# Where the sums of weight blocks are made, and how many pairs are multiplied without them

## The chip, the cores and the metric

The kernel runs on one core of one Trainium2 chip. The metric is the device time of one execution in microseconds (us): the median of several runs. One more execution was taken by the hardware profiler; times of single instructions are from it.

## The reference, cut to what matters

One step of a diffusion network with two layers. The first layer mixes tokens with a state-space scan (SSD), the second with differential attention of eight heads; behind each stands a channel mixer. There are 512 latent and 128 context tokens, so 640 columns in all, and 1024 channels. What this case touches is the channel mixer of the second layer:

```python
def conv_ffn(h, up_w, conv_w, conv_b, down_w):
    u = dwconv(h @ up_w, conv_w, conv_b)
    a, v = jnp.split(u, 2, axis=-1)
    return (jax.nn.silu(a) * v) @ down_w
```

`up_w` is 1024 x 5632: an `a` half and a `v` half of 2816 channels each. `dwconv` is a filter of three taps along the tokens, with a bias for each channel.

## The kernel before, in words

**Products.** Channels lie on the 128 partitions, tokens in the columns. A product of fp32 accuracy is made of three matmuls: weight and activation are each split in a rounded part (`whi`, `h..h`) and the rest (`wlo`, `h..l`), and hi x hi, hi x lo and lo x hi are added in PSUM. `split_w` (L327) makes the two parts of a weight: a copy on ScalarE (L277 is the helper of all ScalarE work), then a subtraction on VectorE (L283 the helper for two-input operations, L280 for those with a scalar as well). L286 is the helper of all matmuls.

**Weights** come in an order that `weight_units` (L1354) lists once for the whole program: units of up to 1024 columns, each loaded in one transfer on SP's queue into one of four `raw` buffers (L306). `nextw` (L332) hands out the next unit; it loads three units ahead and splits one ahead. A unit's split parts lie in one of five pairs of buffers in the second channel mixer.

**The second channel mixer.** A pair is one tile of 128 `a` channels and the tile of the same `v` channels; there are 22. A plain pair is two tiles of 8 contraction blocks x 3 matmuls x two column groups: 96 matmuls of 320 columns on average. From the fifth pair on (`STD = 4`) a pair is computed by class `Blocks` with seven block products in place of eight (Winograd's form): the two tiles of a pair are the rows, two halves of the contraction (four blocks each) the inner dimension, and two halves of the tokens (`HT` = 320 columns) the columns of a 2 x 2 block product. A product is 4 blocks x 3 matmuls, a pair 84 matmuls of 320 columns. Products 1 and 2 take weight blocks as they are, 4 also; 5, 6, 7 and 3 take sums of weight blocks. `product` (L152) runs one product, `pair` (L175) the seven of a pair, of which 3 and 4 are delayed into the next pair (`third`, `fourth`). The epilogue (L757) takes a pair's `ua` and `uv` through the filter, SiLU, product and split (`mh`, `ml`).

**What feeds the products.** The sums of activation blocks (`sums`, L61) are made by VectorE after the first plain pair, a few at a time: `hook` (L258) counts a tick for each contraction block and each block of a product, and lets waiting tasks go on. `finish_sums` (L93) stands after the last plain pair. The four sums of weight blocks of a pair are made by VectorE in `stage` (L119), from the pair's two loaded units; a plan (`plan`, L102) lists the products, and `stage` keeps the splits `LOOK = 7` products ahead of the product that runs.

**The order of the mixer.** Up pairs 0 to 7, the down projection of seven of them, pairs 8 to 14, the next down projection, pairs 15 to 21, the last. In the first of eight down tiles the last pair's products 3 and 4 are run (`between`, L210).

**Attention**, ahead of it, takes three tiles (q, k, v) for each head. `att_evac` (L1181) copies the context part of a head's keys into `kp`, of which there are two buffers; it is stored as an output (`kout`) and used by the head's scores. The head's normaliser goes through DRAM: `rsd` is written and comes back, spread over the partitions, as `rbc` (L400, L402). POOL has no work in this kernel.

Instructions of an engine run in the order in which the program lists them.

Of the kernel before, what the change touches and what calls it, by code (L numbers as in the profile page):

```python
# [41 lines left out]
STD = 4  # L42
HT = T // 2
LOOK = 7
# [5 lines left out]
class Blocks:  # L50


    def __init__(self, st, h, epilogue, pool):
        self.st, self.h, self.epilogue, self.pool = st, h, epilogue, pool
        self.ops = {}
        self.pend = None
        self.spare = None
        self.half = None
        self.units = sorted(st.paired)

    def sums(self):  # L61
# [5 lines left out]
        for j in range(4):  # L67
# [17 lines left out]
            for i, x in ((1, t1), (2, t2), (4, t4)):  # L85
# [3 lines left out]
                st.split_w(t[:, c1], t[:, c2], x)  # L89
# [3 lines left out]
    def finish_sums(self):  # L93
        st, h, t = self.st, self.h, self.t
        self.stage(LOOK)
# [6 lines left out]
    def plan(self, p0, p1):  # L102

        self.seq, self.done, self.at = [], 0, 0
        for p in range(p0, p1):
            prev = p > p0
            self.seq += [(1, p), (2, p)] + [(3, p - 1)] * prev + [(6, p)] + [(4, p - 1)] * prev + [(5, p), (7, p)]
        self.seq += [(0, p1 - 1), (3, p1 - 1), (4, p1 - 1)]

    def place(self):  # L110

        if self.half is None:
            hi, lo = self.st.parts()
            self.half = hi[:, 512:], lo[:, 512:]
            return hi[:, :512], lo[:, :512]
        o, self.half = self.half, None
        return o

    def stage(self, upto):  # L119

        st = self.st
        k1, k2 = slice(0, 512), slice(512, 1024)
        while self.done < min(upto, len(self.seq)):
            i, p = self.seq[self.done]
            self.done += 1
            if i == 0:
                self.half = None
                st.cast(self.units[2 * (p - STD)] + 2)
                continue
            o = self.ops.setdefault(p, {})  # L130
            if i == 1:
                u = self.units[2 * (p - STD)]
                st.prefetch(u + 1)
                x, y = st.wraw[u], st.wraw[u + 1]
                s = [self.pool.tile([P, 512], F32, tag=f"s{n}", name=f"s{n}_{p}", bufs=1) for n in range(1, 5)]
                st.tt(s[0], y[:, k1], y[:, k2], ALU.add)
                st.tt(s[1], s[0], x[:, k1], ALU.subtract)
                st.tt(s[2], x[:, k1], y[:, k1], ALU.subtract)
                o["raw"] = {1: x[:, k1], 2: x[:, k2], 4: y[:, k2], 5: s[0], 6: s[1], 7: s[2], 3: s[3]}
                if self.half is None:  # L140
                    hi, lo = st.parts()
                    st.split_w(hi, lo, x)
                    o[1], o[2] = ((hi[:, k], lo[:, k]) for k in (k1, k2))
            if i == 6:
                st.tt(o["raw"][3], o["raw"][2], o["raw"][6], ALU.subtract)
            if i not in o:
                o[i] = self.place()
                st.split_w(*o[i], o["raw"][i])

    B = {1: "11", 2: "21", 3: "22", 4: 4, 5: 1, 6: 2, 7: 3}  # L150
# [24 lines left out]
    def pair(self, p):  # L175
        st = self.st
        st.wi = self.units[2 * (p - STD)] + 2
        st.prefetch(st.wi + 1)
# [31 lines left out]
    def between(self, i, p0, p1):  # L210

        st = self.st
        if i == 0:
            self.third()
            self.fourth()
            self.half = self.spare = None
            if p1 > p0:
                self.plan(p0, p1)
        if i == 4:
            st.cast(st.wi + 2)  # L220
            self.stage(4)
        if i == 6:
            self.stage(LOOK)


class Step:


    def __init__(self, ctx, tc, a):
# [12 lines left out]
        self.paired = set()  # L242
        self.npart = 0
# [57 lines left out]
    def prefetch(self, upto):  # L301
        while len(self.wraw) <= min(upto, len(self.units) - 1):
            u = len(self.wraw)
            ap, n = self.units[u]
            r = self.pw.tile([P, 1024], F32, tag="raw", name=f"raw{u}", bufs=RAW)
            self.nc.sync.dma_start(r[:, :n], ap)  # L306
            self.wraw[u] = r

    def cast(self, upto):
        while len(self.wcast) <= min(upto, len(self.units) - 1):  # L310
            u = len(self.wcast)
            self.prefetch(u)
            if u in self.paired:
                self.wcast[u] = None
                continue
            n = self.units[u][1]
            hi, lo = (t[:, :n] for t in self.parts())
            self.split_w(hi, lo, self.wraw[u][:, :n])
            self.wcast[u] = hi, lo

    def parts(self):
        v = self.npart
        self.npart += 1
        wp, t, b = (self.pw, "w", 3) if self.px is None or v % 5 < 3 else (self.px, "x", 2)
        return [wp.tile([P, 1024], F32R, tag=t + nm, name=f"w{nm}{v}", bufs=b) for nm in ("hi", "lo")]

    def split_w(self, hi, lo, raw):  # L327

        self.act(hi, raw, AF.Copy)
        self.tt(lo, raw, hi.bitcast(F32), ALU.subtract)  # L330

    def nextw(self):  # L332
# [1183 lines left out]
```

## Time and profile before

| | |
|---|---|
| median of 3 runs | 1886.21 us (1880.86 to 1887.99) |
| the profiled execution | 1884.19 us |
| its span, first to last instruction | 1882.4 us |
| mean granted TensorE clock | 0.991 |
| TensorE (PE) busy | 1841.4 us, 98% |
| VectorE (DVE) busy | 1478.4 us, 79% |
| ScalarE (ACT) busy | 991.6 us, 53% |
| POOL busy | 0.2 us |
| moved by DMA | 209.72 MB, 111 GB/s in the mean |

Times in rows are us from the span's start. Attention stands at about 1060 to 1370, the second channel mixer from about 1390 to the end, its paired stages at 1466 to 1527, 1580 to 1666 and 1719 to 1805. A row of a group of instructions has the line, the engine, the operation, output<-inputs, their sizes and the count, then the busy time and the mean of one in ns, then the idle time ahead of them and what ended it. A row of the timeline has start, duration, engine, line, operation, and in brackets the wait ahead and what ended it. A row of a window has for each engine the busy time and, in brackets, the number of instructions; then the granted clock, the mean busy share of the 16 DMA engines, and what they moved. A row of DMA issues has the count, the size of one, and the median us from issue to landing.

### The profile page before, as it was taken

The page shows a single profiled execution, that of the slowest core. Times are in us where ns is not written, and L with a number is a line of the kernel's source. Part 1 is how long each engine was busy: PE and PEld are TensorE (multiplying, and loading weights), DVE is VectorE, ACT ScalarE, POOL GpSimd, SP SyncE. Part 2 cuts the span into 40 slices and gives each one's busy share as a digit, 9 for nine tenths or more (in the row PEclk, how much of TensorE's full clock was granted, in tenths as well). Part 3 has the DMA queues.
Part 4 walks back from the last instruction along what each step waited for, and adds up shares of the span by engine and source line. Part 5 has one row for each costly group of instructions (what it writes and reads, how often), then busy time and mean ns, then how long its engine had stood idle before and what let it go on. Part 6 is the DMA issues. An engine that isn't in the chain of part 4 may idle for free. (4 is left out here: it accounts for less than half of the span.)

```text
span 1882.4 us, 32863 instructions
## 1 busy us (share of the span) xinstructions
PE 1841.4 (98%) x13117; PEld 1727.3 (92%) x13117; DVE 1478.4 (79%) x2886; ACT 991.6 (53%) x1880; POOL 0.2 (0%) x4
## 2 busy tenths in 40 slices
PE   7999999999999999999999999999999899999997
PEld 4789899989989999999999988888899799999996
DVE  4689999999748999984455877778779885975974
ACT  2479687879336441442343565656546442643651
POOL 0000000000000000000000000000000000000000
PEclk9999999999999999999999999999999899999998
DMA  9735243446543556632222212111031131231221
GB/s 344 256 109 147 92 133 117 117 136 177 186 136 108 190 182 218 188 119 80 77 68 68 88 52 64 47 59 40 23 119 52 55 104 60 73 114 57 68 79 56
DMA packets 79521, 209.72 MB, mean 111 GB/s; under 512 B 9116, under 2 KB 15880, under 8 KB 79240
## 3 DMA queue, kind: packets, MB, share of 16 engines
q1 hardware_dynamic: 78792, 207.10, 34.7%
q8 instruction: 103, 1.69, 0.4%
q10 hardware_dynamic: 576, 0.52, 0.1%
q14 instruction: 50, 0.41, 0.1%
HBM read 201.63 MB, written 5.96 MB: 110 GB/s over the span
## 5 line engine op out<-in xcount | busy, mean ns | idle before, releaser
L277 ACT ACTIVATE whi<-raw 128x1024 fp32r<-128x1024 f32 (+4 forms) x238 | 228.3, 961 | 303.1 <-PE po L286 187.7
L283 DVE TENSOR_TENSOR wlo<-raw,whi 128x1024 fp32r<-128x1024 f32 (+4 forms) x238 | 261.9, 1102 | 79.7 <-ACT whi L277 67.8
L280 DVE SCALAR_TENSOR_TENSOR xr<-po,mod,xr 128x256 f32<-128x256 f32 (+2 forms) x231 | 89.3, 434 | 138.0 <-PE po L286 137.9
L286 PE MATMUL po<-ml,whi 128*128 128x256 f32 (+1 forms) x704 | 168.2, 310 | 0.0
L286 PE MATMUL po<-mh,whi 128*128 128x256 f32 (+1 forms) x704 | 168.0, 310 | 0.0
L286 PE MATMUL po<-mh,wlo 128*128 128x256 f32 (+1 forms) x704 | 167.8, 310 | 0.0
L286 PE MATMUL up<-h01h,wlo 128*128 128x256 f32 (+1 forms) x656 | 149.4, 308 | 0.0
L286 PE MATMUL up<-h01l,whi 128*128 128x256 f32 (+1 forms) x656 | 149.3, 308 | 0.0
L286 PE MATMUL up<-h01h,whi 128*128 128x256 f32 (+1 forms) x656 | 149.3, 308 | 0.0
L286 PEld LDWEIGHTS po<-mh,whi 128*128 128x128 f32 x704 | 128.4, 188 | 0.5 <-ACT mh L277 0.2
L286 PEld LDWEIGHTS po<-mh,wlo 128*128 128x128 f32 x704 | 128.8, 188 | 0.0
L286 PEld LDWEIGHTS po<-ml,whi 128*128 128x128 f32 x704 | 128.6, 188 | 0.1
L286 PEld LDWEIGHTS up<-h01h,wlo 128*128 128x128 f32 x656 | 119.3, 188 | 0.0
L286 PEld LDWEIGHTS up<-h01l,whi 128*128 128x128 f32 x656 | 119.3, 188 | 0.0
L286 PEld LDWEIGHTS up<-h01h,whi 128*128 128x128 f32 x656 | 119.2, 188 | 0.0
L277 ACT ACTIVATE whi<-s 128x512 fp32r<-128x512 f32 x72 | 44.5, 626 | 60.7 <-PE po L286 20.6
L277 ACT ACTIVATE mh<-cv 128x640 fp32r<-128x640 f32 x44 | 32.5, 738 | 79.3 <-DVE cv L283 79.1
L277 ACT ACTIVATE e<-sl,sm 128x640 f32<-128x640 f32 x64 | 50.4, 790 | 40.2 <-DVE sm L1225 39.8
L286 PE MATMUL z<-h00h,whi 128*128 128x256 f32 (+1 forms) x256 | 62.9, 325 | 0.0
L277 ACT ACTIVATE e<-rb,Ctok 128x128 f32<-128x128 f32 x160 | 56.4, 390 | 12.3 <-issue 10.0
L277 ACT ACTIVATE ca<-ca 128x640 f32<-128x640 f32 x44 | 32.4, 736 | 57.0 <-DVE ca L280 56.8
L286 PE MATMUL z<-h00l,whi 128*128 128x256 f32 (+1 forms) x256 | 59.8, 312 | 0.0
(558 smaller groups left out, 5154.7 us busy)
## 6 DMA issues: line engine op xcount, KB each, us to landing
raw<-in_w_up SPq DMA_DIRECT2D x88, 512.0 KB, 3.4
mw<-in_modT SPq DMA_DIRECT2D x48, 512.0 KB, 3.6
raw<-in_w_in SPq DMA_DIRECT2D x40, 512.0 KB, 5.2
rb<-rowd SPq DMA_DIRECT2D x40, 512.0 KB, 5.3
raw<-in_w_dn SPq DMA_DIRECT2D x32, 448.0 KB, 3.4
raw<-in_w_qkv SPq DMA_DIRECT2D x24, 512.0 KB, 3.4
mr<-in_mod SPq DMA_DIRECT2D x44, 256.0 KB, 5.5
raw<-in_w_so SPq DMA_DIRECT2D x16, 512.0 KB, 4.2
```

Of the source, the lines that this page charges most:

```text
L277: return self.nc.scalar.activation(out, in_, func, **k)
L280: return self.nc.vector.scalar_tensor_tensor(out, in0, s, in1, op0, op1)
L283: return self.nc.vector.tensor_tensor(out, a, b, op)
L286: return self.nc.tensor.matmul(out, lhsT, rhs, start=start, stop=stop, **k)
```

## The change

- **Layout.** The up weights of the second layer are stored by blocks of 512 columns (`in_w_blk`: tile, half of the contraction, partition, column). A plain unit is loaded with both halves in one transfer.
- **Sums in DRAM.** A buffer `wsum` in DRAM holds four sums (for products 5, 6, 7, 3) for each of 17 pairs. `weight_sums` makes them with transfers that POOL issues: a copy of one block, then transfers that add a second block to what is there (`accum_op`). It is called once for each of heads 0 to 5 of attention, for three pairs each time (two the last time). Ahead of a batch stand two small transfers that write two numbers of the head's `kp` into the batch's place in `wsum` (marks), so that the batch comes after the head's keys.
- **Signs.** Transfers only add, so the sums have other signs than before. Activation sums are formed with other signs to go with it, those of product 2 are split negated, and the filter taps of the `v` half of the paired tiles are negated, on VectorE, at the start of the mixer.
- **Loads.** A pair's seven blocks come in three and a half units through the same `raw` buffers: 512-column pieces out of `in_w_blk` and `wsum`, in the order in which products use them. `plan`, `place`, `stage` and `parts` are gone; all units are split at 1024 columns, three units ahead (`AHEAD = 3`) within the second mixer.
- **Five plain pairs** (`STD = 5`), 17 paired ones. Matmuls of a product, epilogue and down projections are what they were.

```diff
-STD = 4
+STD = 5
-LOOK = 7
+AHEAD = 3
...
-            st.tt(t1, a[:, c2], a[:, c1], ALU.subtract)
-            st.tt(t2, b[:, c2], t1, ALU.subtract)
-            st.tt(t4, b[:, c1], t2, ALU.subtract)
+            st.tt(t1, a[:, c1], a[:, c2], ALU.subtract)
+            st.tt(t2, b[:, c2], t1, ALU.add)
+            st.tt(t4, t2, b[:, c1], ALU.subtract)
...
-                st.split_w(t[:, c1], t[:, c2], x)
+                st.split_w(t[:, c1], t[:, c2], x, i == 2)
...
-        self.stage(LOOK)
+        st.cast(st.wi + 1)
...
     def product(self, ps, i, p):
         st = self.st
-        self.at += 1
-        self.stage(self.at + LOOK)
-        wh, wl = self.ops[p].pop(i)
+        if self.half is None:
+            hi, lo = st.nextw(AHEAD)
+            wh, wl = hi[:, :512], lo[:, :512]
+            if hi.shape[1] > 512:
+                self.half = hi[:, 512:], lo[:, 512:]
+        else:
+            (wh, wl), self.half = self.half, None
...
-    def nextw(self):
+    def nextw(self, ahead=1):
         u = self.wi
         self.wi += 1
-        self.prefetch(u + 3)
-        self.cast(u + 1)
+        self.prefetch(u + 2 + ahead)
+        self.cast(u + ahead)
...
+            t = cw[:, FT + STD:, 0:3]
+            nc.vector.tensor_scalar(t, t, -1.0, None, ALU.mult)
         self.start_tiles(h)
...
             nc.sync.dma_start(self.a["kout"][hd], kp)
+            if hd < 6:
+                n = -(-(FT - STD) // 6)
+                self.weight_sums(STD + hd * n, min(STD + hd * n + n, FT), kp[0:1, 0:2])
...
+                for p in range(done, end):
+                    prev = p > done
+                    seq += [(1, p), (2, p)] + [(3, p - 1)] * prev + [(6, p)] + [(4, p - 1)] * prev + [(5, p), (7, p)]
...
+    def weight_sums(self, p0, p1, mark):
+
+        g, w, s = self.nc.gpsimd, self.a["w_blk"], self.wsum
+        rows = lambda x: x.rearrange("n p c -> n (p c)").rearrange("n (r c) -> r n c", c=2048)
+        a1, a2, n = slice(p0, p1), slice(FT + p0, FT + p1), slice(p0 - STD, p1 - STD)
+        put = lambda i, x, **k: g.dma_start(rows(s[n, i]), rows(x), **k)
+        add = dict(accum_op=ALU.add)
+        for i in (0, 2):
+            g.dma_start(s[p0 - STD, i, 0:1, 0:2], mark)
+        put(0, w[a2, 0])
+        put(2, w[a1, 0])
+        put(0, w[a2, 1], **add)
+        put(2, w[a2, 0], **add)
+        put(1, s[n, 0])
+        put(1, w[a1, 0], **add)
+        put(3, s[n, 1])
+        put(3, w[a1, 1], **add)
```

Three places show how the change moves instructions. The first is VectorE at the entry to the paired stage, behind the last plain pair. Before (`s_5_` are sums of weight blocks of pair 5, `wlo` splits, `h11l` the last split of activation sums; `ua<-ua,ba` adds product 2 of the first pair):

```order
L283 TENSOR_TENSOR s_5_16295<-raw_16190,raw_16291 128x512
L283 TENSOR_TENSOR s_5_16294<-s_5_16293,raw_16190 128x512
L283 TENSOR_TENSOR wlo_16288<-raw_16190,whi_16287 128x512
L283 TENSOR_TENSOR wlo_16303<-raw_16190,whi_16302 128x512
L283 TENSOR_TENSOR h11l_15409<-T_0_15897,h11h_15408 128x320
L283 TENSOR_TENSOR h11l_15411<-T_0_15897,h11h_15410 128x320
L283 TENSOR_TENSOR h11l_15413<-T_2_16080,h11h_15412 128x320
L283 TENSOR_TENSOR h11l_15415<-T_2_16080,h11h_15414 128x320
L283 TENSOR_TENSOR wlo_16303<-s_4_16272,whi_16302 128x512
L283 TENSOR_TENSOR wlo_16335<-s_5_16294,whi_16334 128x512
L283 TENSOR_TENSOR s_5_16296<-raw_16190,s_5_16294 128x512
L283 TENSOR_TENSOR ua_16316<-ua_16316,ba 128x320
```

In the changed kernel the same place reads:

```order
L225 TENSOR_TENSOR h11l_15470<-T_0_15959,h11h_15469 128x320
L225 TENSOR_TENSOR h11l_15472<-T_0_15959,h11h_15471 128x320
L225 TENSOR_TENSOR h11l_15474<-T_2_16142,h11h_15473 128x320
L225 TENSOR_TENSOR h11l_15476<-T_2_16142,h11h_15475 128x320
L225 TENSOR_TENSOR wlo_16531<-raw_16488,whi_16530 128x1024
L222 SCALAR_TENSOR_TENSOR cv<-uraw,fcw_15636,cv 128x511
L222 SCALAR_TENSOR_TENSOR cv<-uraw,fcw_15636,cv 128x127
L222 SCALAR_TENSOR_TENSOR cv<-uraw,fcw_15636,cv 128x511
L222 SCALAR_TENSOR_TENSOR cv<-uraw,fcw_15636,cv 128x127
L225 TENSOR_TENSOR cv<-ca,cv 128x640
L225 TENSOR_TENSOR ua_16483<-ua_16483,ba 128x320
```

The sums are gone and one wide split stands in place of four narrow ones; the filter of the last plain pair now stands between the last split and the add into `ua`.

The second place is POOL, which had only four MEMSETs before. This is the stretch from the marks of heads 2 and 3 to those of heads 4 and 5 (each `kp` row is two marks of one head; `x4` counts transfers in a row):

```order
L1364 DMA wsum<-kp_12391 2x1x1 x2
L1364 DMA wsum<-kp_12828 2x1x1 x2
L1361 DMA wsum<-in_w_blk 32x3x2048 x2
L1361 DMA wsum<-wsum 32x3x2048
L1361 DMA wsum<-in_w_blk 32x3x2048 x4
L1361 DMA wsum<-wsum 32x3x2048
L1361 DMA wsum<-in_w_blk 32x3x2048 x3
L1361 DMA wsum<-wsum 32x3x2048
L1361 DMA wsum<-in_w_blk 32x3x2048 x3
L1361 DMA wsum<-wsum 32x3x2048
L1364 DMA wsum<-kp_13264 2x1x1 x2
L1364 DMA wsum<-kp_13700 2x1x1 x2
```

The batches of two heads are mixed, their marks go first, and 16 large transfers stand between one pair of marks and the next.

The third place is SP, with the weight loads of the paired stage. Before, two units of 1024 columns for each pair:

```order
L306 DMA raw_16190<-in_w_up 128x1024
L306 DMA raw_16291<-in_w_up 128x1024
L306 DMA raw_16398<-in_w_up 128x1024
L306 DMA raw_16400<-in_w_up 128x1024
L306 DMA raw_16542<-in_w_up 128x1024
```

In the changed kernel:

```order
L251 DMA raw_16252<-in_w_blk 128x2x512
L251 DMA raw_16336<-wsum 128x512 x2
L251 DMA raw_16394<-wsum 128x512
L251 DMA raw_16394<-in_w_blk 128x512
L251 DMA raw_16485<-in_w_blk 128x512
L251 DMA raw_16485<-wsum 128x512
L251 DMA raw_16488<-wsum 128x512
L251 DMA raw_16488<-in_w_blk 128x512
L251 DMA raw_16491<-wsum 128x512 x2
```

Each unit of 1024 columns is now two pieces of 512, of which a sum comes out of `wsum` and a plain block out of `in_w_blk`, and a pair takes three and a half units.

More of the change, by code (lines that the diff above doesn't have):

```diff
@@ L119, in stage @@
[L119 to L148, printed above, removed]
@@ L797, in ffn @@
                 self.drain(self.modtask)
-            after = blk and (lambda i: blk.between(i, done, min(sub[s + 1][1] + 1, FT) if not last else done))
             if not last:
-                self.project_out(mid, range(k0, k1), self.gate(l, 1), after=after)
+                self.project_out(mid, range(k0, k1), self.gate(l, 1), after=blk and blk.between)
             else:
                 self.project_last(mid, range(k0, k1), self.gate(l, 1), nextnorm, parts="CD" if l else "AB",
-                                  after=after)
+                                  after=blk and blk.between)
     def ssd_consts(self, pool):
```

122 lines of the change are left out of this document (59 added, 63 removed).

## The prediction

> **What bounds the kernel now.** Start with the page: who is busy, and at what clock.
>
> ```profile
> PE 1841.4 (98%) x13117; PEld 1727.3 (92%) x13117; DVE 1478.4 (79%) x2886; ACT 991.6 (53%) x1880; POOL 0.2 (0%) x4
> ```
>
> TensorE is the bound, POOL is free, VectorE has a fifth to spare on average. An average hides stages, so next come the windows of the second channel mixer, cut where its plain pairs end and the seven-product pairs begin (about 1466), with two stretches from elsewhere for the DMA load.
>
> ```profile
> core 0: us, PE busy (x) PEld busy (x) DVE busy (x) ACT busy (x) POOL busy (x), PEclk, DMA share, GB/s
> 1436.00:1466.00 30.00, 30.00 (x207) 30.00 (x205) 30.00 (x60) 20.85 (x36) 0.00 (x0) 1.00 0.12 36
> 1466.00:1494.00 28.00, 20.72 (x96) 18.20 (x95) 21.55 (x38) 8.97 (x17) 0.00 (x0) 0.76 0.17 57
> 1494.00:1527.00 33.00, 32.53 (x217) 31.73 (x218) 30.71 (x57) 21.71 (x37) 0.00 (x0) 1.00 0.35 101
> ...
> 1580.00:1666.00 86.00, 85.39 (x570) 83.15 (x568) 77.61 (x139) 53.04 (x91) 0.00 (x0) 1.00 0.26 78
> 1719.00:1805.00 86.00, 85.39 (x569) 83.17 (x568) 77.76 (x139) 53.23 (x91) 0.00 (x0) 1.00 0.26 82
> ...
> 0.00:47.00 47.00, 36.72 (x404) 22.77 (x404) 20.19 (x45) 13.19 (x23) 0.20 (x4) 1.00 0.96 344
> 1162.00:1274.00 112.00, 111.90 (x745) 96.38 (x743) 85.13 (x173) 66.97 (x143) 0.00 (x0) 1.00 0.18 55
> ```
>
> Before 1466 VectorE is full: 30.00 of 30 us. Then TensorE falls to 96 matmuls in 28 us at a clock of 0.76. What ends its waits stands in the timeline of TensorE:
>
> ```profile
> 1463.80 0.46 PE L286 MATMUL up<-h11h,whi 128*128 128x256 f32 x2
> ...
> 1465.26 0.46 PE L286 MATMUL up<-h11h,wlo 128*128 128x256 f32 x2
> ...
> 1469.17 0.42 PE L286 MATMUL ba<-h11h,wlo 128*128 128x320 f32 x1 [1.84 <-DVE wlo L283]
> ...
> 1481.91 0.56 PE L286 MATMUL ba<-T,whi 128*128 128x320 f32 x2 [2.07 <-DVE ua L283]
> ```
>
> From 1463.80 to 1465.26 ten matmuls start in 1.46 us: **0.146 us** each, the undisturbed rate. The 96 of the 28 us should take 14.0, so **14.0 us are lost** at the entry to the paired stage, behind VectorE. By the same rate 33 - 217 x 0.146 = 1.3, 86 - 570 x 0.146 = 2.8 and 86 - 569 x 0.146 = 2.9 us are lost in the rest of the paired stage. That is all there is to win; elsewhere nothing is changed that TensorE waits for.
>
> **The change part by part.**
>
> *A fifth plain pair.* Pair 4 takes 96 matmuls of 320 columns on average instead of 84: 12 x 0.146 = **+1.75 us**, whatever else happens.
>
> *The sums of weight blocks leave VectorE.* These groups are of the stretch 1465 to 1815, all of it on VectorE:
>
> ```profile
> L283 DVE TENSOR_TENSOR wlo<-s,whi 128x512 fp32r<-128x512 f32 x72 | 48.7, 687 | 9.6 <-ACT whi L277 9.6
> ...
> L283 DVE TENSOR_TENSOR wlo<-raw,whi 128x1024 fp32r<-128x1024 f32 x14 | 17.1, 1223 | 2.6 <-ACT whi L277 2.6
> ...
> L283 DVE TENSOR_TENSOR s<-raw,s 128x512 f32<-128x512 f32 x18 | 12.4, 688 | 0.1
> ```
>
> Four sums of 0.688 us go from each pair, 2.75 us; seven narrow splits (7 x 0.687 = 4.8) become three and a half wide ones (3.5 x 1.223 = 4.3). So 3.2 us of VectorE go from each 12.3 us of pair (84 x 0.146).
>
> *The entry.* The sums of activation blocks run on ticks, 38 of them after the first pair. Plain tiles gave 40 ticks before the paired stage and now give 56, so VectorE has the fifth pair's time to catch up. What is late next is the first pair's own chain. The rows that price it:
>
> ```profile
> 1466.02 0.69 ACT L277 ACTIVATE uraw<-up 128x640 f32<-128x640 f32 x1
> 1467.13 0.92 ACT L277 ACTIVATE cv<-uraw,fcw 128x640 f32<-128x640 f32 x1
> ...
> 1469.03 1.93 DVE L280 SCALAR_TENSOR_TENSOR cv<-uraw,fcw,cv 128x511 f32<-128x511 f32 x4
> 1471.47 0.82 DVE L283 TENSOR_TENSOR cv<-ca,cv 128x640 f32<-128x640 f32 x1
> 1481.38 0.48 DVE L283 TENSOR_TENSOR ua<-ua,ba 128x320 f32<-128x320 f32 x1
> ...
> 1484.27 1.06 ACT L277 ACTIVATE whi<-raw 128x1024 fp32r<-128x1024 f32 x1 [6.76 <-PE ba L286]
> ```
>
> In the new order the last plain tile is followed on ScalarE by one wide split (1.06), the copy (0.69) and the tap (0.92), then on VectorE by the convolution (1.93), the product (0.82) and the add into `ua` (0.48): 5.9 us. Product 6 waits for that add, as at 1481.91, and now has 37 matmuls ahead of it, 5.4 us. So 0.5 us stay, and 0.9 for the small waits that the paired stage shows anyway: 14.0 - 1.4 = **-12.6 us**. Bounds: -14.0 if nothing stays; -6 if VectorE is still late by half of what it was.
>
> *The later paired stages.* VectorE is busy 77.6 of 86 us there; with a quarter of it gone the lookahead stays full. Of 2.8 + 2.9 us I take **-2.0**; bounds 0 and -5.7. Splitting three units ahead replaces a lookahead of seven products, three and a half units; nothing for that.
>
> *More weight bytes.* Seven blocks instead of four: 1.75 MB per 12.3 us is about 149 GB/s, in pieces of 256 KB. The first window shows 344 GB/s at a share of 0.96, so 43% of the engines. Four raw buffers are filled ahead; cost nothing, and a few us if a load ever took over 10 us.
>
> *The sums in DRAM.* POOL issues, in six batches, 8 transfers for three pairs each, 768 KB apiece: 17 x 8 x 256 KB = 35.7 MB, half of them additions. No transfer from POOL, none within DRAM and no addition stands in this trace, so the cost is bounded by loads:
>
> ```profile
> raw<-in_w_qkv SPq DMA_DIRECT2D x17, 512.0 KB, 3.4
> ...
> raw<-in_w_ao SPq DMA_DIRECT2D x3, 128.0 KB, 2.3
> ...
> x<-in_xT SPq DMA_DIRECT2D x8, 320.0 KB, 5.9
> ...
> rbc<-rsd SPq DMA_DIRECT2D x11, 320.0 KB, 3.2
> ```
>
> From 128 to 512 KB is 1.1 us, so 768 KB land in 4.1 us, and an addition that moves twice the bytes in 6.3: 5.2 us on average. At 344 GB/s the bytes fill the engines for 104 us, or 155 if an addition counts double. Spread from about 1060 to 1350 that is 36 to 54% on top of the 18% in the attention window: loaded, not full. Who feels it is the one transfer in attention with little slack:
>
> ```profile
> 1192.16 0.50 SPq L400 DMA_DIRECT2D rsd<-rs_y  x1
> ...
> 1193.76 0.33 SPq L402 DMA_DIRECT2D rbc<-rsd  x1
> ...
> 1197.93 0.88 DVE L280 SCALAR_TENSOR_TENSOR o<-o,sg,rbc 128x640 f32<-128x640 f32 x1
> ...
> 1201.30 0.88 DVE L280 SCALAR_TENSOR_TENSOR w<-e,sm,e 128x640 f32<-128x640 f32 x1
> ...
> 1202.55 0.27 PE L1288 MATMUL wt<-cst,w 128*128 128x128 f32 x1
> ```
>
> `rbc` is used 4.2 us after its issue and lands after 3.2: 1.0 us of slack. If it is late, VectorE stands, and behind the operation wait `ql`, the rotation of `k` and `w`, whose transpose TensorE takes 0.4 us after `w` ends. In the full first 47 us a load of the same 320 KB landed after 5.9, so at worst it is 2.7 - 1.0 = 1.7 us late in six heads: +10 us. At best 0. At half to three quarters of the load I take 0.5 a head, **+3**. The Trainium skill (DMA: Bandwidth & Descriptors, "Issuing engines are not separate DMA queues") speaks against the change here: transfers issued by GpSimd interleave with those of SP on the same 16 engines. By it the term is not 0; whether it is 3 or 10 it doesn't say.
>
> *Small things.* A sign change of 51 filter taps on VectorE waits for `fcw`:
>
> ```profile
> 1368.76 0.33 SPq L748 DMA_DIRECT2D fcw<-in_fcw  x1
> ...
> 1373.12 1.14 DVE L280 SCALAR_TENSOR_TENSOR xr<-po,mod,xr 128x256 f32<-128x256 f32 x3 [2.76 <-PE po L286]
> ```
>
> Its load goes out at 1368.76, and VectorE idles anyway until 1373.12, for TensorE; nothing. Negated splits cost what splits cost.
>
> Sum: +1.75 - 12.6 - 2.0 + 3 = **-9.9 us**. It is made against the profiled execution (1884.19 around a span of 1882.4), which lies 2.0 under the median of the runs shown. The same difference from the median 1886.21 gives **1876**.
>
> **The rivals.**
>
> *POOL comes too late (slower).* These two rows are the places:
>
> ```profile
> 1161.84 0.27 ACT L277 ACTIVATE kp<-k 128x128 f32<-128x128 f32 x1
> ...
> 1273.72 0.27 ACT L277 ACTIVATE kp<-k 128x128 f32<-128x128 f32 x1
> ```
>
> POOL's order has 16 large transfers between the marks of heads 2 and 3 (not before 1161.84, when head 3's `kp` exists) and the marks of head 4. There are two `kp` buffers, so head 6's `kp`, at 1273.72, waits on ScalarE until head 4's marks have read theirs, and behind it wait `e`, `wTh` and the splits, so TensorE. That leaves 111.9 / 16 = 7.0 us a transfer. At 5.2, one after the other, 83 us go and 29 are spare; some run two at a time. From 7 us on each further us costs 16: at 8.3 us +21, less the 9.9 won: **1897**. For it: nothing here shows an addition's speed. Against: the spare third.
> The Trainium skill (SBUF — State Buffer, "SBUF: two separate sides") states how it could come: GpSimd writes these descriptors through a port that VectorE can hold, and a transfer of about 620 ns then took about 3100. An estimate by the Trainium skill's page, 5.2 + 2.5 = 7.7 us, would be 11 us late: about 1887; of the chance of this rival, a third is for this way. Its section "Who interferes with whom" spares two-input operations against writes, which are most of attention's; no row here can show it.
>
> *Attention gives it back (no change).* `rbc` late by 1.7 us in six heads: -2.9 in all, **1883**. For it: 1.0 us of slack and a direct path to TensorE. Against: the engines don't fill.
>
> *The entry stays slow (no change).* If the first pair waits for the last plain pair's epilogue longer than 0.5 us, half the 14.0 stays: -4, **1882**. For it: the add still stands behind that convolution. Against: no 30 us of backlog.
>
> **How the numbers follow.** Half a per cent, 9.4 us, is about what a measurement of this kernel can tell from no change. Forecast 0.58, its own range 1868 to 1881: 0.46 of it is faster by more than that, 0.12 within. POOL late 0.19 (0.17 slower, 0.02 same). Attention 0.14 and entry 0.09, same. So faster 0.46, same 0.37, slower 0.17. The range: best case -14.0 - 5.7 + 1.75 = -18 with a little scatter, 1867, up to the POOL case, 1897.
>
> **What would show it.** Right: between the last plain tile and the second pair TensorE has no idle over 1 us and no half clock; VectorE's `s` rows are gone, and the paired windows hold 0.146 to 0.149 us a matmul; `o<-o,sg,rbc` starts within 5 us of `rbc`'s issue; the last POOL transfer lands before 1369. Wrong: ScalarE waiting at a `kp` copy for a DMA, `rbc` landing after 5 us or more, SP's `raw` issues shifted in attention, or a wait on `ua` of over 2 us at the entry.

## The result, and the profile after

The changed kernel is slower: 1893.25 us (median of 13 runs, 1886.71 to 1898.47) against 1882.36 us before (13 runs, 1880.83 to 1887.99). The ratio is 1.0052, 95% interval 1.0039 to 1.0065. The forecast was 1876, 9.9 us less than the median it was made from; measured are 10.9 us more. So the sign was wrong. The time lies inside the range, close to the 1897 of the slower rival, but that is luck: what this rival described did not happen (below).

The page of the profile after (1893.15 us, span 1891.3) has VectorE with 47 us less work than before, the new queue with its 35.66 MB, and its transfers. Those of 768 KB out of `in_w_blk` land after 6.9 us in the median, and all 48 large ones after 6.3 on average, where 5.2 was estimated:

```profile
PE 1843.0 (97%) x13129; PEld 1729.4 (91%) x13129; DVE 1431.0 (76%) x2759; ACT 985.1 (52%) x1825; POOL 41.8 (2%) x64
...
q0 software_dynamic: 5504, 35.66, 8.0%
...
wsum<-in_w_blk POOLq DMA_DIRECT2D x30, 768.0 KB, 6.9
```

To see where the time went, both traces are cut at three points that each kernel has: head 0's copy to `kp`, the first matmul `up<-` of the second mixer, and the last matmul of the first paired stage. In the timeline of the changed kernel, on ScalarE and TensorE, they are:

```profile
1063.75 0.29 ACT L219 ACTIVATE kp<-st 128x128 f32<-128x128 f32 x1
...
1449.35 0.47 PE L228 MATMUL up<-h11h,whi 128*128 128x256 f32 x2
...
1543.61 0.31 PE L228 MATMUL ba<-T,wlo 128*128 128x320 f32 x1
```

The same three points of the kernel before (the last is a `bb<-T,wlo` there) are at 1060.12, 1430.34 and 1536.43.

| stretch | before | after | difference |
|---|---|---|---|
| start to head 0's `kp` | 1060.1 | 1063.8 | +3.6 |
| attention and the first tile of the mixer, to the first `up<-` | 370.2 | 385.6 | **+15.4** |
| plain pairs and first paired stage | 106.1 | 94.3 | **-11.8** |
| all that follows, to the end of the span | 346.0 | 347.7 | +1.8 |

**The entry** won what it was to win. The windows are those of the prediction: the last 30 us of plain pairs, the first paired stage, and the two later ones.

```profile
core 0: us, PE busy (x) PEld busy (x) DVE busy (x) ACT busy (x) POOL busy (x), PEclk, DMA share, GB/s
...
1469.00:1499.00 30.00, 30.00 (x206) 30.00 (x206) 29.75 (x56) 19.32 (x31) 0.00 (x0) 1.00 0.29 88
1498.60:1534.00 35.40, 34.71 (x229) 33.26 (x228) 25.05 (x40) 20.72 (x30) 0.00 (x0) 1.00 0.37 105
1587.00:1673.00 86.00, 85.41 (x566) 82.79 (x565) 64.93 (x102) 50.87 (x73) 0.00 (x0) 1.00 0.42 129
1726.00:1812.00 86.00, 85.41 (x567) 82.78 (x566) 64.71 (x101) 50.74 (x73) 0.00 (x0) 1.00 0.44 132
```

There is no stretch at half clock any more: 229 matmuls in 35.4 us lose 35.4 - 229 x 0.146 = 2.0 us. VectorE is still full up to the entry (29.75 of 30), but TensorE hardly waits behind the last plain pair any more. The two waits that the timeline names in this stage are short:

```profile
1510.37 0.56 PE L228 MATMUL ba<-T,whi 128*128 128x320 f32 x2 [0.53 <-ACT uv L219]
...
1514.31 0.41 PE L228 MATMUL bb<-h11h,whi 128*128 128x320 f32 x1 [0.16 <-ACT ua L219]
```

In the later paired stages VectorE has 13 us less to do in 86, and TensorE is not faster for it: 566 and 567 matmuls where 570 and 569 stood before.

**Attention** gave it back. First what VectorE and TensorE waited for there (columns: total us, times, longest), then the timeline of one head on SP, VectorE and TensorE:

```profile
DVE o L222 <- DMA rbc<-rsd: 11.9, 4, 3.5
...
PE wt L1231 <- ACT wpT L219: 5.4, 2, 2.9
PE wt L1231 <- DVE w L222: 2.8, 1, 2.8
```

```profile
1194.27 0.33 SPq L251 DMA_DIRECT2D raw<-in_w_qkv  x1
1196.41 0.50 SPq L342 DMA_DIRECT2D rsd<-rs_y  x1
...
1201.58 0.33 SPq L344 DMA_DIRECT2D rbc<-rsd  x1
...
1205.76 0.88 DVE L222 SCALAR_TENSOR_TENSOR o<-o,sg,rbc 128x640 f32<-128x640 f32 x1 [3.51 <-DMA rbc<-rsd]
...
1208.52 0.85 PE L1231 MATMUL wt<-cst,w 128*128 128x128 f32 x3 [2.91 <-ACT wpT L219]
```

`rbc` cannot be issued before `rsd`, 2.5 KB, has landed. Before, 1192.16 to 1193.76, that took 1.6 us; here 5.2. `rbc` itself took longer too: VectorE, which waits for it, starts 4.2 us after its issue, where it landed after 3.2 in the row of before. VectorE stands 3.5 us, and 2.8 us after `o<-` starts, TensorE, which has stood 2.9 us, gets its `wt`. The head before it shows the same chain with POOL idle: POOL issues nothing from 1141.19 until head 3's marks at 1166.65, and `rsd` at 1159.12 is followed by `rbc` at 1160.70, as before the change.

```profile
1141.19 1.10 POOL L1364 DMA_DIRECT2D wsum<-kp  x2
1166.65 1.03 POOL L1364 DMA_DIRECT2D wsum<-kp  x2 [24.36 <-ACT kp L219]
...
1159.12 0.50 SPq L342 DMA_DIRECT2D rsd<-rs_y  x1
...
1160.70 0.33 SPq L344 DMA_DIRECT2D rbc<-rsd  x1
```

Over the seven heads from `rsd` to `rbc`: 1.6 us each before; 4.7, 1.6, 5.2, 3.0, 1.9, 5.0, 1.6 after. From `rbc`'s issue to the start of `o<-`, in the four heads in which VectorE waits for it: 4.9, 4.2, 5.9 and 3.5 us. Matmul by matmul the two traces move apart at four `wt`, by 1.7, 3.0, 2.5 and 2.9 us: 10.1 of the 15.4. Most of the rest, 1.4 to 1.5 us each time, comes right behind the last three of them, where the granted clock is lower (the first window is the stretch up to the wait above, the second what follows it, the other two what follows the third and the fourth). Behind the first one, of 1.7 us, the clock stays at 1.00 from 1137 to 1154, and nothing more is lost:

```profile
1170.00:1208.00 38.00, 35.57 (x237) 30.57 (x235) 25.53 (x54) 21.72 (x46) 4.34 (x6) 1.00 0.78 197
1208.00:1225.00 17.00, 16.44 (x92) 13.12 (x93) 9.97 (x19) 6.72 (x15) 2.06 (x3) 0.90 0.75 209
...
1249.80:1266.00 16.20, 16.12 (x91) 12.89 (x91) 9.27 (x17) 6.25 (x13) 3.62 (x6) 0.90 0.67 169
...
1331.00:1348.00 17.00, 16.84 (x99) 14.91 (x100) 15.18 (x28) 10.95 (x23) 2.32 (x3) 0.90 0.53 120
```

Some 2 us more come up around head 6's `kp`, which stands later in the program's order: 56.7 us behind head 5's, where it was 37.3 before (run 11 comes back to this). Early in the attention the changed kernel gains 1.2 us.

The +3.6 of the start come before any changed instruction. Over the other profiled runs with the same code there, head 0's `kp` lies between 2.5 earlier and 2.9 later than before, so this is scatter, though a little beyond what those runs show. The entry of the kernel before also scatters: two runs below with the same code there took 103.9 us, not 106.1. The medians differ by 10.9 us, and the typical sum is: attention +15 to +21 (below), entry about -9.6, and about +1 for all that follows (346.0 to 346.7 us in the three profiled runs with the mixer of before, 346.9 to 348.3 in the nine with the changed one).

### The profile page after: what moved, and what is told of

Its sections match the earlier page's. It is cut to its first block, busy times and chain, and to the rows that moved or that the text cites. A ratio compares the mean times of both kernels' runs of the same rounds, so it can differ in the third digit from the quotient of the medians.

```text
span 1891.3 us, 33002 instructions
## 1 busy us (share of the span) xinstructions
PE 1843.0 (97%) x13129; PEld 1729.4 (91%) x13129; DVE 1431.0 (76%) x2759; ACT 985.1 (52%) x1825; POOL 41.8 (2%) x64
## 3 DMA queue, kind: packets, MB, share of 16 engines
q0 software_dynamic: 5504, 35.66, 8.0%
## 4 chain that ended last, share of the span: by engine, by line
PE 89%; DVE 4%; DMA 4%; ACT 2%; issue 1%; SPq 0%; DVEq 0%; ACTq 0%
PE po L228 25%; PE up L228 18%; PE z L228 6%; PE x L228 5%; PE bc L228 5%; PE ba L228 5%; PE bb L228 5%; PE st L228 4%; PE yp L228 3%; PE v L228 2%; PE q L228 2%; PE ov L228 1%; PE sl L228 1%; PE wt L1231 1%; ACT e L219 1%; DMA rbc<-rsd 1%
## 5 line engine op out<-in xcount | busy, mean ns | idle before, releaser
L219 ACT ACTIVATE whi<-raw 128x1024 fp32r<-128x1024 f32 (+4 forms) x257 | 261.9, 1020 | 362.9 <-PE po L228 225.4
L225 DVE TENSOR_TENSOR wlo<-raw,whi 128x1024 fp32r<-128x1024 f32 (+4 forms) x257 | 301.6, 1174 | 101.7 <-ACT whi L219 91.6
L228 PE MATMUL z<-h00h,wlo 128*128 128x256 f32 (+1 forms) x256 | 59.7, 312 | 0.0
```

The source lines that it names most:

```text
L219: return self.nc.scalar.activation(out, in_, func, **k)
L225: return self.nc.vector.tensor_tensor(out, a, b, op)
L228: return self.nc.tensor.matmul(out, lhsT, rhs, start=start, stop=stop, **k)
```

## The experiments

Times are medians; ratios are to the kernel before, run on the same chip in between, with 95% intervals. "Attention" and "entry" are the second and third stretch of the table above, in the profiled execution. That one lies within 2.5 us of the median, but for three runs: in runs 3 and 7 it is the fastest of all (1878.23 and 1871.76), in run 5 the slowest (1881.13).

| run | us | ratio | attention | entry |
|---|---|---|---|---|
| before | 1882.36 | | 370.2 | 106.1 |
| changed kernel | 1893.25 | 1.0052 (1.0039 to 1.0065) | 385.6 | 94.3 |
| 1: before + unread sums | 1902.56 | 1.0106 (1.0093 to 1.0119) | 390.4 | 103.9 |
| 2: changed, later `o` | 1870.16 | 0.9933 (0.9920 to 0.9946) | 368.8 | 94.3 |
| 3: changed, sums in the first mixer | 1883.41 | 1.0008 (0.9996 to 1.0021) | 369.0 | 94.3 |
| 4: changed, small transfers | 1911.74 | 1.0160 (1.0147 to 1.0173) | 391.0 | 94.3 |
| 5: before, five plain pairs | 1877.15 | 0.9968 (0.9957 to 0.9979) | 370.1 | 100.4 |
| 6: later `o`, four plain pairs | 1876.19 | 0.9965 (0.9952 to 0.9979) | 365.7 | 100.4 |
| 7: before, later `o` | 1876.24 | 0.9961 (0.9948 to 0.9973) | 361.9 | 103.9 |
| 8: later `o`, two units ahead | 1871.74 | 0.9941 (0.9928 to 0.9954) | 366.6 | 94.3 |
| 9: changed, `rsd` from ScalarE | 1892.03 | 1.0046 (1.0030 to 1.0062) | 391.1 | 94.3 |
| 10: changed, four `kp` | 1890.47 | 1.0041 (1.0026 to 1.0057) | 387.4 | 94.3 |
| 11: later `o`, four `kp` | **1867.38** | 0.9918 (0.9903 to 0.9932) | 361.7 | 94.3 |
| 12: before, later `o`, five plain pairs | 1869.97 | 0.9931 (0.9919 to 0.9943) | 361.8 | 99.4 |
| 13: changed, four `kp`, small marked transfers | 1903.40 | 1.0102 (1.0085 to 1.0119) | 399.1 | 94.3 |

### 1. The transfers alone

To the kernel before, `wsum` and `weight_sums` of the changed kernel are added, and `in_w_blk` as one more input:

```diff
             nc.sync.dma_start(self.a["kout"][hd], kp)
+            if hd < 6:
+                n = -(-(FT - 5) // 6)
+                self.weight_sums(5 + hd * n, min(5 + hd * n + n, FT), kp[0:1, 0:2])
```

> The kernel before, with the changed kernel's transfers in DRAM added to its attention (same sums, same marks, same six batches); nothing reads the sums, VectorE goes on making its own. Theory A (the load of the DMA engines delays the small transfer rsd and then rbc; VectorE stands at o<-o,sg,rbc, and TensorE behind it): the attention loses what it lost in the changed kernel, 15.4 us (10 in four waits at wt, 5 in a lower clock), so 11 to 19 us slower than before, with rsd to rbc at 2 to 5 us in place of 1.6. Rival B (the loss came with the new order of instructions or the loads of 512 columns, not with the transfers): within 4 us of before.

Measured: 19.2 us slower by the medians (1883.35 before, taken in between), attention 390.4 in place of 370.2, `rsd` to `rbc` 3.5 to 5.0 us in five heads of seven. VectorE's wait, and TensorE's (first row VectorE, the others TensorE):

```profile
DVE o L280 <- DMA rbc<-rsd: 14.5, 5, 4.4
...
PE wt L1288 <- ACT wpT L277: 8.9, 3, 3.8
PE wt L1288 <- DVE w L280: 2.6, 1, 2.6
```

So the transfers by themselves make the loss; the new loads and the new order of the second mixer are not needed for it. At +20.2 it is larger than the 15.4 of the changed kernel's profiled run; runs 9 and 10 have +20.8 and +17.2.

### 2. The waiting operation later

```diff
-            bc = yield from self.rms_spread(pool, [sq], P, 9)
-        self.stt(o, o, self.sg[:, hd // 7:hd // 7 + 1], bc[:, :T], ALU.mult, ALU.mult)
+            bc = yield from self.rms_spread(pool, [sq], P, 20)
+        g = self.sg[:, hd // 7:hd // 7 + 1]
+        if hd < 6:
+            g0, g = g, pool.tile([P, 1], F32, tag="sgl", name="sgl", bufs=2)
+            self.stt(g, self.klast[:, :1].bitcast(F32), 0.0, g0, ALU.mult, ALU.add)
+        self.stt(o, o, g, bc[:, :T], ALU.mult, ALU.mult)
...
             k = self.att_k(k, hd, pool)
+            self.klast = k[1]
```

The added operation is 0 x (one column of the next `kl`) + the gain: it changes no value, and holds `o<-` back until that `kl` exists. The 20 in place of 9 is the number of ticks after which the head's task goes on.

> The changed kernel, with o<-o,sg,rbc of heads 0 to 5 tied to the next k, so that it stands about ten operations (7 us) later on VectorE; transfers as in the changed kernel. Theory A: rbc is late as before, but nothing waits for it: 9 to 15 us faster than the changed kernel, about 1878 to 1884. Rival C (the transfers hurt in another way: kp copies, weight loads, SBUF): within 4 us of the changed kernel, 1889 to 1897.

Measured: 1870.16, 23 us faster than the changed kernel and 12 faster than the kernel before, more than any theory said. POOL's transfers run as they did (65% of the engines in the attention, as in the changed kernel), and `rsd` is as slow, 6.1 us in this head, but there is work ahead of `o<-`:

```profile
1192.96 0.50 SPq L342 DMA_DIRECT2D rsd<-rs_y  x1
...
1199.04 0.33 SPq L344 DMA_DIRECT2D rbc<-rsd  x1
...
1201.30 0.88 DVE L222 SCALAR_TENSOR_TENSOR w<-e,sm,e 128x640 f32<-128x640 f32 x1
...
1206.26 0.15 DVE L222 SCALAR_TENSOR_TENSOR sgl<-kl,sg 128x1 f32<-128x1 f32 x1
1206.45 0.89 DVE L222 SCALAR_TENSOR_TENSOR o<-o,sgl,rbc 128x640 f32<-128x640 f32 x1
```

The wait at `o<-` falls from 11.9 us to 1.2. That rules out rival C in the form given. Why more came back than had been lost, runs 7 and 11 show: the later place is worth something by itself.

### 3. The sums in the first mixer

```diff
                     pair(done)
+                    if not l and done % 3 == 1 and done < 17:
+                        n = -(-(FT - STD) // 6)
+                        q = STD + done // 3 * n
+                        self.weight_sums(q, min(q + n, FT), mid[done][0].bitcast(F32)[0:1, 0:2])
...
-            if hd < 6:
-                n = -(-(FT - STD) // 6)
-                self.weight_sums(STD + hd * n, min(STD + hd * n + n, FT), kp[0:1, 0:2])
```

> The changed kernel, with the six batches issued in the first channel mixer (after its pairs 1, 4, 7, 10, 13 and 16, marks taken from mh), where no transfer goes through DRAM and back to VectorE. Theory A: attention is as fast as before the change and the entry keeps its 11.8 us: 1871 to 1878. Rival D (a load on the DMA engines costs wherever it stands, through late weight or modulation loads): 1884 or more, with waits on raw or mr in the first mixer.

Measured: 1883.41, no faster than before; the median is nearer to rival D. The profiled execution is the fastest of 12, 5 us under the median, so it shows only a part of what the median lost. In it attention is at 369.0, but the stretch from the first mixer's first matmul to head 0's `kp` grew from 468.1 to 476.3 us. The windows show where (the 30 us of the second row held 208 matmuls before), and the second fence VectorE's wait from 740 to 780:

```profile
592.00:747.00 155.00, 153.08 (x1043) 152.82 (x1041) 141.12 (x243) 62.19 (x75) 17.28 (x25) 1.00 0.84 261
745.00:775.00 30.00, 23.97 (x160) 23.23 (x160) 25.42 (x47) 4.51 (x5) 1.46 (x2) 1.00 0.85 261
775.00:1060.00 285.00, 284.61 (x1990) 282.52 (x1989) 189.94 (x358) 112.73 (x155) 23.19 (x33) 1.00 0.58 168
```

```profile
DVE junk L667 <- DMA mw<-in_modT: 7.7, 4, 3.4
```

VectorE stood for modulation rows (`mw`) that came late, 19.0 us in the whole of this mixer where it was 1.3 before, and TensorE waited for what VectorE and ScalarE had behind them. This mixer's own traffic already holds 0.6 to 0.7 of the engines there, and 0.85 with the sums. From 775 on, with a share of 0.58, TensorE loses almost nothing. So here, too, the load cost where VectorE waits for a transfer in its line.

### 4. Smaller transfers, and 13, the same with marks

```diff
-        put = lambda i, x, **k: g.dma_start(rows(s[n, i]), rows(x), **k)
+        def put(i, x, **k):
+            for r in range(0, 32, 8):
+                g.dma_start(rows(s[n, i])[r:r + 8], rows(x)[r:r + 8], **k)
```

> The changed kernel, each transfer of POOL cut into four of a quarter of the rows (192 KB in place of 768), same bytes, same place. If the small rsd waits behind the transfer in flight (theory A, as a queue), its way takes a quarter of the extra 0.3 to 3.6 us and the loss of 15.4 falls below 8: 1879 to 1886. If it is the share of the engines that decides, whatever the size of the pieces, 1889 to 1898.

Measured: 1911.74, slower by 18, but for a reason that the run was not made for. A mark orders only the place in `wsum` that it writes. Three of four pieces held no mark, and POOL began them at once:

```profile
1.32 1.89 POOL L1364 DMA_DIRECT2D wsum<-in_w_blk  x3 [0.88 <-POOLq L1499]
```

60 of them ran in the first 160 us, and the first mixer began 16.2 us later than before. As a test of the queue it is inconclusive. Run 13 repeats it with a mark for each piece, and four buffers for `kp` (run 10):

```diff
         for i in (0, 2):
-            g.dma_start(s[p0 - STD, i, 0:1, 0:2], mark)
+            for r in range(0, P, 32):
+                g.dma_start(s[p0 - STD, i, r:r + 1, 0:2], mark)
```

> The changed kernel with four buffers for kp, each transfer of POOL cut in four (192 KB), and a mark for every piece, so that no piece starts ahead of its head; to be compared with the run that has four buffers for kp and whole transfers (1890.5). If rsd waits for what is in flight at the moment (its extra 0.3 to 4 us go with the size of a piece): rsd to rbc under 2.5 us and 5 to 12 us faster, 1879 to 1886. If it is the share of the engines that POOL's transfers hold, whatever their size: 1887 to 1895, or slower where more transfers take longer in all.

Measured against run 10: `rsd` to `rbc` at 1.6 to 4.1 us, mean 2.6 over seven heads, in place of 3.6; VectorE's wait at `o<-` 8.5 us in place of 15.5; and the way from head 0's `kp` to the last head's `obc` 11.5 us longer than before, in place of 17.3. That looks as if the size of what is in flight had a part in it, but it isn't shown: the other runs with whole transfers in attention have means of 2.7 to 3.5 us from `rsd` to `rbc`, and here the same bytes are spread over 108 us more. The run is slower all the same (1903.40): POOL is busy for 167 us, not 42, to issue 240 transfers, and the last one starts at 1460, 108 us later than in run 10. And the sign change that was to cost nothing is waited for (first two rows SP, the third VectorE):

```profile
1399.71 46.35 SPq L251 DMA_DIRECT2D raw<-in_w_blk  x7
1446.36 0.34 SPq L690 DMA_DIRECT2D fcw<-in_fcw  x1
...
1452.84 0.19 DVE L720 TENSOR_SCALAR fcw<-fcw 128x51 f32<-128x51 f32 x1 [4.50 <-DMA fcw<-in_fcw]
```

In run 10 the load of the taps (`fcw`) goes out at 1386.74, ahead of these weight loads; here it stands behind seven of them in SP's order. The last marks had been issued by 1419.3, so it does not wait for them at that time. Why the program's order puts it there was not tried.

### 5 and 6. What the entry owes to each part

Run 5 changes one number of the kernel before, run 6 the same number of run 2:

```diff
-STD = 4
+STD = 5
```

```diff
-STD = 5
+STD = 4
```

> The kernel before with five plain pairs in place of four; VectorE goes on making the sums of weight blocks. Theory E (the entry lost its 14 us because VectorE makes the first pairs' weight sums there, and the fifth pair alone gives it only part of the time to catch up: a plain pair is 14.1 us, of which its own work takes some 7): about 7 of the 14 us stay, +1.8 for the matmuls, so 3 to 7 us faster than before. Rival F (the fifth pair does it all, the weight sums need not leave VectorE): 10 to 13 us faster, as much as the changed kernel gains at its entry.

> The changed kernel with o<-o,sg,rbc later (the run before that was faster than both), with four plain pairs. Theory E: without the weight sums VectorE is behind by some 6 us at the entry (14 less about 8 for twelve sums), less 1.8 for fewer matmuls: 2 to 6 us slower than with five pairs, about 1872 to 1876. Rival G (with the weight sums gone nothing is behind, the fifth pair only costs its matmuls): 1 to 2 us faster, 1868 to 1869.

Measured: run 5 is 5.6 us faster than before, run 6 6.0 us slower than run 2, at the edge of what was expected. Both entries take 100.4 us, half-way between 106.1 and 94.3. The first row is the first paired stage of run 5, the second that of run 6; each still has a stretch of lower clock that the changed kernel hasn't:

```profile
1481.00:1523.00 42.00, 37.66 (x232) 36.02 (x231) 32.54 (x58) 21.16 (x36) 0.00 (x0) 0.92 0.24 70
```

```profile
1462.00:1515.00 53.00, 47.60 (x297) 45.60 (x296) 39.47 (x63) 28.68 (x42) 0.00 (x0) 0.94 0.41 124
```

So theory E holds: neither part does it alone, and each gives about half (about a third, if the 103.9 us of runs 1 and 7 are taken for the entry of before).

### 7. The later place in the kernel before

The edit is that of run 2.

> The kernel before with o<-o,sg,rbc of heads 0 to 5 tied to the next k, as in the changed kernel's variant. Nothing waited at it before, so within 3 us of before; if the later place were a gain by itself (and not the slack that the transfers use up), 5 us faster or more.

Measured: 6.5 us faster, with attention at 361.9 in place of 370.2. Nothing had waited for `rbc` at `o<-`, so the expectation, within 3 us, was wrong. The three heads between the `kp` of head 3 and of head 6 take 111.88 us before (1161.84 to 1273.72) and 106.73 here. The same windows, first of before, then of this run, have the same matmuls in less time, with no idle to be seen in either:

```profile
1161.80:1273.70 111.90, 111.80 (x743) 96.30 (x742) 85.03 (x172) 66.87 (x142) 0.00 (x0) 1.00 0.18 55
```

```profile
1159.60:1266.40 106.80, 106.80 (x744) 95.42 (x743) 85.81 (x174) 67.16 (x143) 0.00 (x0) 1.00 0.18 58
```

From one start to the next instruction's, an `sl` takes 0.114 us in the mean of a head in place of 0.131, and an `ov` 0.267 in place of 0.298. With `o<-` later, `ql` comes 0.8 us earlier, and TensorE's list has the `wt` and `ov` between `v` and `q` where they stood between `sl`. Which of the two makes the gain wasn't tried apart.

### 8. Less lookahead

```diff
-AHEAD = 3
+AHEAD = 2
```

> The variant with o<-o,sg,rbc later, with weights split two units ahead in place of three in the second mixer. If three units are more than the epilogue of a pair takes on VectorE (4 to 6 us, a unit is 3.5), two (7 us) do nearly as well: 0 to 3 us slower, 1870 to 1873. If the lookahead carries the paired stage: over 6 us slower, with waits of TensorE on wlo.

Measured: 1871.74, within the scatter of run 2, entry and paired stages the same to 0.1 us. Two units are enough here.

### 9. `rsd` on another queue

```diff
-        self.nc.sync.dma_start(d.rearrange("(j n) -> j n", j=4), y.rearrange("(j r) n -> j r n", r=32)[:, 0, :])
+        q = self.nc.scalar if wait == 9 else self.nc.sync
+        q.dma_start(d.rearrange("(j n) -> j n", j=4), y.rearrange("(j r) n -> j r n", r=32)[:, 0, :])
```

> The changed kernel, with the small transfer rsd of attention issued by ScalarE in place of SP; rbc stays on SP. Theory H (rsd waits in SP's queue behind a weight load, and this load is what POOL's transfers make slow: 7.5 us in place of 3.35): rsd to rbc falls to 2.2 us or less, the waits at o<-o,sg,rbc to under 2 us in all, and 8 to 13 us come back, 1880 to 1886. Rival I (rsd is slow because it shares the engines with POOL's transfers, whatever its queue): rsd to rbc stays at 2 to 5 us, 1890 to 1897.

Measured: 1892.03, attention 391.1: no gain. `rsd` to `rbc` is 1.7, 1.6, 5.3, 3.4, 5.0, 2.8, 1.6 us, as on SP. One head, on ScalarE's queue, SP and VectorE:

```profile
1230.29 0.50 ACTq L343 DMA_DIRECT2D rsd<-rs_y  x1
...
1233.64 0.33 SPq L345 DMA_DIRECT2D rbc<-rsd  x1
...
1240.12 0.88 DVE L222 SCALAR_TENSOR_TENSOR o<-o,sg,rbc 128x640 f32<-128x640 f32 x1 [3.99 <-DMA rbc<-rsd]
```

Theory H falls: the weight load ahead of `rsd` in SP's queue is not what holds it. In this head `rbc` is the later of the two: 6.5 us from its issue to `o<-`. The Trainium skill (DMA: Bandwidth & Descriptors, "Issuing engines are not separate DMA queues") has it so: what the engines issue shares the same 16 engines. The run agrees, on a transfer of 2.5 KB.

### 10 and 11. Four buffers for `kp`

```diff
-        p = pool.tile([P, TP], F32, tag=f"{name}p", name=f"{name}p{hd}", bufs=2)
+        p = pool.tile([P, TP], F32, tag=f"{name}p", name=f"{name}p{hd}", bufs=4)
```

> The changed kernel with four buffers for kp (and qp) in place of two, so that no copy to kp waits for marks; the order of TensorE in attention is then that of the kernel before. If the marks' hold on kp is part of the attention's loss (in the variant with a later o, 5 us came up between the kp of heads 5 and 7): 3 to 6 us faster than the changed kernel, 1887 to 1890. If all of it is rbc: within 2 us, 1891 to 1895.

> The variant with o<-o,sg,rbc later, and four buffers for kp. With the two costs of the transfers in attention both gone: 3 to 6 us faster than that variant, 1864 to 1867. If the marks cost nothing: 1869 to 1872.

Run 10: 1890.47, 2.8 us under the changed kernel, between the two expectations, with intervals that overlap (1.0026 to 1.0057, and 1.0039 to 1.0065). Its attention still costs 17.2 us over before, with the order of TensorE that the kernel before had, and `o<-` waits 15.5 us: the marks' hold on `kp` is not what makes the loss.

Run 11 is the fastest of all: 1867.38, 0.82% under the kernel before (interval 0.68 to 0.97%). Its attention takes 361.7 us, as much as that of run 7 without any transfer, 361.9. So with slack at `o<-`, and with no `kp` held, 35.7 MB of transfers in the attention cost TensorE nothing, at two thirds of the engines:

```profile
1064.00:1364.00 300.00, 296.34 (x2004) 259.02 (x2003) 236.43 (x480) 182.38 (x380) 40.39 (x58) 1.00 0.67 171
```

Run 2 lacks 7 us of this in the profiled executions, 2.8 by the medians. There, with two buffers, the copy of head 6's `kp` and the matmuls behind it stand later in the order, and 5 us come up between the `kp` of heads 5 and 7.

### 12. No transfers at all

The edits are those of run 7 and `STD = 5`.

> The kernel before with the later o<-o,sg,rbc and with five plain pairs, and no transfers in DRAM at all; VectorE makes the sums of weight blocks. If the two gains add (6.5 and 5.6 us): 1869 to 1873, as fast as the changed kernel with the later o. If they overlap: 1874 to 1877.

Measured: 1869.97. The gains add. Sums that VectorE makes, five plain pairs and the later `o<-` are as fast as run 2. Run 11 differs from it by the sums in DRAM (and the buffers): its entry is 5.1 us shorter, its later paired stages 0.8 longer, its ratio 0.9918 against 0.9931, and these two intervals overlap. What the sums in DRAM are worth, once they collide with nothing, is 2.6 us by the medians and at most some 5, not clear of the noise.

## Why the prediction was wrong

- **The sums in DRAM: +3, at worst +10.** This is the step that failed; it measured +15.4, and +17 to +21 in runs 1, 9 and 10. Place and path were named rightly: `rbc`, then `o<-`, then `ql`, `k`, `w`, then `wt`. The size was off for three reasons. Only `rbc`'s own landing was priced, with 1.7 us of lateness at worst; but `rsd`, put at nothing, goes ahead of it through the same engines, and took up to 5.2 us in place of 1.6. `rbc` came late as well: 3.5 to 5.9 us where VectorE waited for it, and one head reached the 5.9 that was its bound. The engines were as full as estimated in the mean (0.64 from 1062 to 1370, for 54 to 72%), but 0.78 and 0.75 around the wait shown above. And a wait costs more than its length: behind three of the four a lower clock added 1.4 to 1.5 us. Among the signs listed, those on `rbc` (5 us from its issue) showed in one head only, with 5.9; `rsd` was not on the list.
- **The rival "attention gives it back"** is what happened, with 0.14 of the chance. It was put at 1883, no change, because it carried the same 1.7 us. That was no bound: it came from a load of 320 KB in a busy window, and the chain has two transfers.
- **"POOL comes too late"**, the rival on the slower side, is not what happened: no engine but POOL waited for a mark, and around head 6's `kp` only the 2 us named above were lost. From the first transfer behind head 3's marks, at 1168.55, to head 4's marks at 1254.45, 16 transfers took 86 us: 5.4 each, with their overlap, where 5.2 was the estimate and 7.0 the limit. The last one started at 1358.5. With four times as many transfers (run 13) the last one started 108 us later than in run 10. The Trainium skill's way to it (SBUF — State Buffer, "SBUF: two separate sides"), descriptors held up by VectorE, doesn't show: no issue of a large transfer on POOL took over 0.94 us in the changed kernel.
- **The entry: -12.6 + 1.75 = -10.9.** Right: -11.8 measured in the same profiled executions. 2.0 us stayed, where 0.5 + 0.9 were worked out. One caution: the stretch of before scatters by 2.2 us, and against 103.9 it would be -9.6. Runs 5 and 6 show that the reason was right too: the backlog that the weight sums and the missing fifth pair leave on VectorE. So the rival "the entry stays slow" is out.
- **The later paired stages: -2.0.** Wrong, though small: +0.4 each. VectorE lost a sixth of its 77.6 us there, not a quarter, but that is not why. Of the 2.8 and 2.9 us that TensorE loses there, nothing is VectorE's. Before and after, 20 to 24 matmuls at the start of a product come up to 0.25 us after the one ahead of them instead of 0.146, and one of them 0.9, behind a `ua` on ScalarE. What makes the 0.25 stays open.
- **"That is all there is to win; elsewhere nothing is changed that TensorE waits for."** Wrong: run 7 found 8.3 us in attention (6.5 by the medians), in windows in which TensorE showed next to no idle time.
- **More weight bytes, lookahead, the signs: nothing.** Right: SP's loads held, run 8 with less lookahead is as fast, and the sign change waits for nobody in the changed kernel.

## What to carry to other kernels

Before a change puts load on the DMA engines, list the transfers that an engine waits for in line, and price the whole chain of each, small transfers included, not the largest one: here 2.5 KB, written to DRAM and read back, cost some 1%. Give that wait slack first, by a later place in the order; with it, and with buffers enough that the marks hold up nothing, the same load was free. And an engine that reads as busy throughout can still run the same instructions faster in another order: compare instructions per us, not busy time.

## What the runs showed of the hardware

- A transfer of 2.5 KB to DRAM is done after 1.6 us without transfers from POOL, and after up to 5.2 us (changed kernel), 6.5 (run 11) beside transfers of 768 KB from POOL; issued by ScalarE, after up to 5.3 (run 9). With transfers of 192 KB it was 4.1 at most (run 13). The 320 KB read back behind it landed after 3.2 us before; where VectorE waited for them, its operation started 3.5 to 5.9 us after their issue in the changed kernel, and up to 7.3 in run 10.
- Additions into DRAM land after 7.0 us for 768 KB (median of 24; those of the last batch are 512 KB), copies from the input after 4.8 (median of 12), copies within `wsum` after 5.7 (12). POOL is busy about 0.9 us to issue an addition and 0.6 for a copy.
- Cutting the transfers in four did not help in all: POOL's time to issue rose from 42 to 167 us, and the last one started 108 us later (run 13 against run 10).
- Behind three waits of TensorE of 2.5 to 3.0 us in attention the granted clock was 0.90 over the 16 to 17 us that followed; behind one of 1.7 us it was 1.00 (changed kernel).
